# Side work of a hybrid Fourier and neighbourhood-attention block: stepped three times where it was four times, and two MLP weight jobs moved to the last gates

## The chip, the cores and the metric

The kernel runs on one core of a Trainium2 chip. The metric is device time in microseconds (us) of one execution; the time before is the median of three runs. TensorE is called PE, its weight loads PEld, VectorE DVE, ScalarE ACT, GpSimd POOL and SyncE SP. SP computes nothing: it issues most of the DMAs, one after the other, and each of them waits at the head of that queue for what it needs.

## The reference, cut to what matters

One transformer-like layer over 2048 latent tokens of width 1024, with 256 context tokens. Six modulation rows come from `silu(c) @ w_ada + b_ada` (and a second set from `c_ctx` for the context tokens).

```python
hx = modulate(rms_norm(x, norm1_g), sh1, sc1)        # hc: the same for ctx
f, q, k, v = split_projection(hx @ w_in)             # four parts of 512 columns
y_four = fourier_mix(f)                              # 2-D FFT over tokens and channels
y_attn = neighbourhood_attention(q, k, v, kc, vc, rpb)
mixed  = gated_merge(hx, y_four, y_attn, w_gate, w_fo, w_ao, w_o)   # sigmoid(hx @ w_gate)
x = x + g1 * mixed
x = x + g2 * ((relu(modulate(rms_norm(x, norm2_g), sh2, sc2) @ w_mlp1) ** 2) @ w_mlp2)
```

`w_mlp1` is 1024 by 4096 and `w_mlp2` 4096 by 1024, 16 MB each in fp32.

## The kernel before, in words

fp32 products are made from fp16 halves: an operand is scaled and split into a high and a low fp16 part, and three products (high-high, high-low, low-high) are summed in PSUM (`mm3`, line 77; its matmuls all have line 82).

**The input stage** multiplies `hx` (four blocks of 512 tokens, kept in SBUF) by `w_in` and `w_branch_gate`. Their columns come in units of 256, and the units in eight pairs (`seq`): pair 0 the Fourier columns f; pair 1 gates 4 and 5; pair 2 q0 with g0; pair 3 q1 with g1; pair 4 both v units; pair 5 k0 with g2; pair 6 k1 with g3; pair 7 the last gates, g6 and g7. `run_pair` (line 767) goes through a pair block by block, and for k and v through the context tokens too. Pair 3 begins with the building of `hc` from the context tokens. A gate or f unit makes two groups of 24 matmuls of 512 columns for each block, a q, k or v unit four groups of 24 matmuls of 256 columns. PSUM holds four such groups (`mmp`). A gate group is emptied by ACT (sigmoid, `ot_g`), a v group by ACT (`vo`, two buffers, stored to `vF`), a q or k group by ACT and DVE (norm and rotary: `ss`, `qn`, `t`, `qr`; POOL makes `rs`), then transposed on PE (`tq`) and split (`sH` on ACT, `sL` on DVE). The weights of the next pair are loaded and split beside the running one (`load_unit`).

**The side work** is written as Python generators whose steps are strewn between the groups. After every group `tick(share)` (line 457) adds `pace` to a counter, and for every 2 in the counter takes one step of each generator in `beside`:

```python
ticks[0] += pace[0]
with tc.issue_after(last_load[0].ins):
    while ticks[0] >= 2:
        ticks[0] -= 2
        for o in beside:
            if next(o, o) is o and o is side:
                blocks[2] = True
```

`issue_after` puts the DMAs of those steps behind the last load of x or of input weights in SP's queue; it orders nothing else. The order of instructions on every engine is made when the program is built: a scheduler goes by a simulated timeline, and takes the earliest in program order of those that it holds for ready. So a step can run ahead of, or behind, the group that it was written beside.

`side_work` (line 294) makes these steps: eight blocks of the context's modulation rows, two steps each and one more (1 to 17), eight of the second modulation (18 to 33), eight chunks of the gates' rows g1 and g2 (34 to 49), three tables of the attention's bias (50 to 52: `wm`, `tT`), 32 loads of 1 MB of the MLP weights (`w12m`, 53 to 84), and two steps that make scales from them (`msd`, `msc`); the 87th call finds it at its end. A modulation block or chunk is a 1 MB load (`awt`, two buffers), eight or so DVE instructions (`ada_sum`, lines 274 to 277) and one or two small matmuls on PE (`adc`, `adm`, `adg`). Of the 32 loads `w12m`, which use the same two buffers, DVE takes the maximum of the first 16 (line 338), ACT the sum of squares of the other 16 (line 340).

When `side` is at its end, `tick` also adds up `share` (1.5 for a gate group, 0.8 for v, 0.6 for q or k) and for each whole 1 takes a step of `early_blocks`: MLP weight jobs by `prepare` (line 389). A job loads 1 MB of `w_mlp1` or `w_mlp2` (`raw`), forms seven sums and differences of its quarters (DVE, line 430), halves each into two fp16 parts (ACT line 386, DVE line 387, the tile `wo`) and stores 1.75 MB to `w1d` or `w2d` in DRAM: one step to begin with, seven for each job, and the call that finds the end. There are 32 jobs; `N_EARLY` of them, eight, are done here, four of `w_mlp1` and then four of `w_mlp2`, and the MLP stage does the other 24.

After pair 4 `split_values` (v split into halves, line 838, 19 calls) joins `beside`. Ahead of pair 7 what is left of all of these is run to its end, the buffers `pb` are given back, and `beside` becomes `fourier_prep` (line 866): tables and norms for the Fourier and output weights (`tw`, `wn`, through two buffers `wst`) and two folds of f, 25 steps and the call that finds the end. What pair 7 leaves of it is run behind the pair. Then come the channel and token DFTs, the attention, the output projection and the MLP.

Of the kernel before, what the change touches and what calls it, by code (L numbers as in the profile page):

```python
# [8 lines left out]
F32 = mybir.dt.float32  # L9
F32R = mybir.dt.float32r  # L10
F16 = mybir.dt.float16
# [11 lines left out]
KT = D // 128  # L23
# [40 lines left out]
def dit_block(ctx: ExitStack, tc: tile.TileContext, a, out, taps=None, upto=9):  # L64
    nc = tc.nc
    act, dve, pool, pe, sp = nc.scalar, nc.vector, nc.gpsimd, nc.tensor, nc.sync
# [110 lines left out]
    pa = sbuf("p1a", "right")  # L177
# [116 lines left out]
    def side_work():  # L294
# [75 lines left out]
        dve.tensor_scalar(out=AB2, in0=AB2, scalar1=msc[:, 1:2], scalar2=None, op0=ALU.mult)  # L370
        dve.tensor_scalar(out=g2r, in0=g2r, scalar1=msc[:, 4:5], scalar2=None, op0=ALU.mult)

    def early_blocks():

        yield from prepare(jobs[:N_EARLY], lambda n_: pb.tile([128, KT, 256], F32, tag="awt", name=n_, bufs=2).rearrange("p k n -> p (k n)"),
                           lambda n_: pb.tile([128, 2, 256], F32, tag="aacc", name=n_, bufs=2).rearrange("p a n -> p (a n)"),
                           lambda n_: pb.tile([128, D], F32, tag="xh", name=n_, bufs=5).bitcast(F16).rearrange("p (c n) -> p c n", c=2),
                           2, sp.dma_start, sp.dma_start)
        del jobs[:N_EARLY]


    prepared, N_EARLY = set(), 8
    jobs = [(kind, f + o) for f in range(0, FF // 128, 8) for kind in (1, 2) for o in range(0, 8, 2)]

    def halve(hi, lo, src, scale):
# [65 lines left out]
    beside, pace = [side], [0]  # L451

    ticks = [0]
# [3 lines left out]
    def tick(share):  # L457

        ticks[0] += pace[0]
        with tc.issue_after(last_load[0].ins):  # L460
            while ticks[0] >= 2:
                ticks[0] -= 2
                for o in beside:
                    if next(o, o) is o and o is side:
                        blocks[2] = True

            if blocks[2]:
                blocks[1] += share
                while blocks[1] >= 1.0:
                    blocks[1] -= 1.0  # L470
                    next(blocks[0], None)
# [217 lines left out]
    seq = [f_, g_[4:6], (q_[0], g_[0]), (q_[1], g_[1]), v_, (k_[0], g_[2]), (k_[1], g_[3]), g_[6:8]]  # L689
# [75 lines left out]
        return r  # L765

    def run_pair(n):
        pace[0] = 3 if n == len(seq) - 1 else (0, 3, 2)[min(n, 2)]
        wu, new = pair(n), [load_pair_unit(n + 1, u) for u in range(2)] if n + 1 < len(seq) else []
        js = [0, 1, "c", 2, 3] if n else [1, 2, 3]  # L770
        for j in js:
# [94 lines left out]
    def fourier_prep():  # L866
        fold(0)
        yield
        for i in range(4):
            tH, tL = (fb.tile([128, 4, 512], F32R, tag=f"t{o}{i}", name=f"t{o}{i}") for o in "HL")  # L870
            tabs.append((tH, tL))

            tw = pa.tile([128, 4, 512], F32, tag="wst", name=f"tw{i}", bufs=2)
            sp.dma_start(tw, a["seq"][i].rearrange("(j p) m -> p j m", p=128))
            for j in range(4):
                split_on((pool, dve)[j % 2], tH[:, j], tL[:, j], tw[:, j])
                yield
            for j in (2 * i, 2 * i + 1):
                w, k = ((a["w_attn_out"][0], j), (a["w_out"][0], j - 2), (a["w_fourier_out"][0], j - 6))[(j >= 2) + (j >= 6)]
                tn = pa.tile([128, 2, D], F32, tag="wst", name=f"wn{j}", bufs=2)  # L880
                sp.dma_start(tn, w[k * 256:(k + 1) * 256, :].rearrange("(k p) n -> p k n", p=128))
                tn = tn.rearrange("p k n -> p (k n)")
                act.activation(tn, tn, AF.Square, accum_out=wn[:, j:j + 1])
                yield
        fold(1)

    for n in range(len(seq)):
        if n == 1:
# [6 lines left out]
        if n == len(seq) - 1:  # L895
# [7 lines left out]
            fb = sbuf("ffb")  # L903
# [960 lines left out]
```

## Time and profile before

| | |
|---|---|
| median of 3 runs | 2662.83 us (2658.7 to 2666.41) |
| the profiled execution | 2660.88 us, of which the span from first to last instruction is 2659.1 us |
| busy, share of the span | PE 2538.6 us (95%), DVE 1827.3 (69%), ACT 1183.3 (44%), POOL 484.4 (18%) |
| granted PE clock, mean | 0.985 |
| input stage, pairs 1 to 7 | about 157.6 to 838 us of the span |
| DFTs, attention and the rest | 838 to 2659.1 us |

All times of single instructions below are from that one profiled execution. An engine's idle time counts only where PE, or what ends last, waits for it. A "tick" below is one call of `tick`, so one group of matmuls.

### The profile page before, as it was taken

The page shows a single profiled execution, that of the slowest core. Times are in us where ns is not written, and L with a number is a line of the kernel's source. Part 1 is how long each engine was busy: PE and PEld are TensorE (multiplying, and loading weights), DVE is VectorE, ACT ScalarE, POOL GpSimd, SP SyncE. Part 2 cuts the span into 40 slices and gives each one's busy share as a digit, 9 for nine tenths or more (in the row PEclk, how much of TensorE's full clock was granted, in tenths as well). Part 3 has the DMA queues.
Part 4 walks back from the last instruction along what each step waited for, and adds up shares of the span by engine and source line. Part 5 has one row for each costly group of instructions (what it writes and reads, how often), then busy time and mean ns, then how long its engine had stood idle before and what let it go on. Part 6 is the DMA issues. An engine that isn't in the chain of part 4 may idle for free.

```text
span 2659.1 us, 42665 instructions
## 1 busy us (share of the span) xinstructions
PE 2538.6 (95%) x15830; PEld 1473.0 (55%) x15830; DVE 1827.3 (69%) x3672; ACT 1183.3 (44%) x2113; POOL 484.4 (18%) x715
## 2 busy tenths in 40 slices
PE   6899989898999899998999999999999999999999
PEld 5445756776656678875666444444444444444444
DVE  6756976568553678887777696978877644636367
ACT  5623225545242577874444564627351333314050
POOL 1201221012224545452000121121211100000000
PEclk9999999999999999998999999999999999999999
DMA  8577689867374744556767777787766533333334
GB/s 269 137 225 204 203 248 304 270 204 245 93 249 141 199 118 138 148 169 207 237 226 264 260 242 261 231 279 233 268 235 230 181 99 105 101 103 99 104 103 155
DMA packets 345962, 517.77 MB, mean 195 GB/s; under 512 B 48497, under 2 KB 210505, under 8 KB 341401
## 3 DMA queue, kind: packets, MB, share of 16 engines
q1 hardware_dynamic: 296425, 406.50, 48.8%
q0 software_dynamic: 29104, 75.23, 8.4%
q10 hardware_dynamic: 20224, 33.31, 3.9%
q8 instruction: 124, 2.03, 0.3%
q14 instruction: 85, 0.70, 0.1%
HBM read 370.11 MB, written 145.84 MB: 194 GB/s over the span
## 4 chain that ended last, share of the span: by engine, by line
PE 68%; DMA 11%; DVE 11%; issue 3%; ACT 3%; POOL 3%; SPq 2%; DVEq 0%; ACTq 0%; POOLq 0%
PE p L82 21%; PE pm L82 17%; PE ps_g L82 8%; PE po L82 6%; DMA w12m<-in_w_mlp 3%; PE pua L82 2%; PE ps_k L82 2%; PE tp L1325 2%; PE pmf L1263 2%; PE pv L1339 1%; SPq L188 1%; PE ps_f L82 1%; PE ps_v L82 1%; PE sc L1303 1%; DVE wo L387 1%
## 5 line engine op out<-in xcount | busy, mean ns | idle before, releaser
L82 PE MATMUL pm<-hc,wb 128*128 128x512 f16 x2688 | 582.6, 379 | 5.6 <-DVE p L1605 2.1
L82 PE MATMUL p<-wb,a 128*128 128x512 f16 x2688 | 581.9, 379 | 2.1 <-DVE X L1605 1.5
L82 PEld LDWEIGHTS <-wb 128*128 128x128 f16 x2688 | 262.9, 98 | 323.6 <-issue 7.3
L82 PEld LDWEIGHTS <-a 128*128 128x128 f16 x2688 | 263.0, 98 | 319.7 <-issue 2.9
L82 PE MATMUL ps_g<-hx,w_g 128*128 128x512 f16 x1536 | 342.5, 380 | 0.9 <-ACT ot_f L516 0.9
L1605 DVE TENSOR_TENSOR X<-X,p 128x512 f32<-128x512 f32 x280 | 184.5, 685 | 171.1 <-PE p L82 151.8
L82 PEld LDWEIGHTS <-hx 128*128 128x128 f16 x2304 | 227.4, 99 | 39.6 <-issue 7.2
L82 PEld LDWEIGHTS <-w_g 128*128 128x128 f16 x1536 | 151.0, 99 | 171.2 <-issue 3.2
L1091 POOL DMA_DIRECT2D bt<-tT x264 | 132.4, 508 | 76.3 <-DVE ri L1332 53.0
L1605 DVE TENSOR_TENSOR u<-pm,u 128x512 f32<-128x512 f32 x128 | 87.5, 690 | 84.3 <-PE pm L82 82.5
L1312 DVE CUSTOM_DVE_ANT_0 s<-sc,bt,qsc 128x736 f32<-128x736 f32 (+5 forms) x128 | 111.2, 869 | 37.1 <-PE sc L1306 33.9
L386 ACT ACTIVATE wo<-ws,msc 128x512 f16<-128x512 f32 x96 | 69.0, 718 | 152.0 <-DVE ws L430 124.0
L1609 ACT ACTIVATE p<-pm 128x512 f32<-128x512 f32 x32 | 18.9, 589 | 239.7 <-PE pm L82 239.7
L1739 POOL DMA_DIRECT2D xr<-x1d x32 | 17.3, 539 | 569.8 <-DVE X L1605 562.1
L1333 DVE SCALAR_TENSOR_TENSOR pL<-tp,pH 128x640 f16<-128x640 f32 (+1 forms) x128 | 112.3, 878 | 5.0 <-ACT pH L1328 4.5
L1316 ACT ACTIVATE s<-s,m 128x736 f32<-128x736 f32 (+5 forms) x128 | 104.6, 817 | 16.5 <-DVE m L1312 13.9
L386 ACT ACTIVATE wo<-raw,msc 128x512 f16<-128x512 f32 x128 | 87.4, 709 | 52.0 <-DVE raw L430 17.8
L82 PE MATMUL po<-wouH,mH 128*128 128x512 f16 x256 | 97.3, 384 | 9.3 <-DVE ga L1383 9.3
L1325 PE MATMUL tp<-ident,s 128*128 128x128 f32 x704 | 103.1, 281 | 0.8 <-ACT s L1316 0.7
L516 ACT ACTIVATE ot_g<-ps_g,usc_g 128x512 f32<-128x512 f32 x64 | 43.4, 681 | 130.9 <-PE ps_g L82 117.6
L82 PE MATMUL po<-wouL,mH 128*128 128x512 f16 x256 | 98.8, 386 | 2.4 <-POOL wouL L1536 2.4
L387 DVE SCALAR_TENSOR_TENSOR wo<-raw,msc,wo 128x512 f16<-128x512 f32 x128 | 94.4, 748 | 8.0 <-ACT wo L386 7.9
(535 smaller groups left out, 4645.9 us busy)
## 6 DMA issues: line engine op xcount, KB each, us to landing
wb<-w1d SPq DMA_DIRECT2D x224, 256.0 KB
wb<-w2d SPq DMA_DIRECT2D x224, 256.0 KB
w12m<-in_w_mlp SPq DMA_DIRECT2D x32, 1024.0 KB
raw<-in_w_mlp ACTq DMA_DIRECT2D x24, 1024.0 KB
w1d<-wo POOLq DMA_DIRECT2D x84, 256.0 KB, 4.0
w2d<-wo POOLq DMA_DIRECT2D x84, 256.0 KB, 4.0
gT<-ot_g SPq DMA_DIRECT2D x64, 256.0 KB
hc<-hcd SPq DMA_DIRECT2D x14, 1024.0 KB
```

Source lines behind the costliest of these rows:

```text
L82: last_mm[0] = pe.matmul(ps, l, r, start=(start and i == 0), stop=(stop and i == n - 1))
L188: last_load[0] = sp.dma_start(dst, src)
L386: act.activation(hi, src, AF.Copy, scale=scale)
L387: dve.scalar_tensor_tensor(out=lo, in0=src, scalar=scale, in1=hi, op0=ALU.mult, op1=ALU.subtract)
L516: act.activation(o, ps, func, scale=scale)
L1091: load_(t[i * 16:(i + 1) * 16, :, off + j0 * w:off + (j0 + 8) * w], raw(tT[ct], (2 * hp * 15 + dr) * w, [[120 * w, 16], [15 * w, 2], [1, 8 ...
L1263: pe.matmul(ps, l, r, start=(i == 0), stop=(i == len(prods) - 1))
L1312: tail["dve"] = dve.tensor_tensor_reduce(out=s[:, :n], in0=sc, in1=bias, op0=ALU.add, op1=ALU.min, scale=qsc[:, 4:5], scalar=3.0e38, accum ...
L1316: tail["act"] = act.activation(s[:, :n], s[:, :n], AF.Exp, bias=m1[:, 0:1], scale=-1.0, accum_out=m1[:, 1:2])
L1325: tail["pe"] = pe.transpose(tp[:, i * 128:(i + 1) * 128], s[:, o:o + 128], ident)
L1333: tail["dve"] = dve.scalar_tensor_tensor(out=pL[:, :c], in0=tp[:, :c], scalar=PTOP, in1=pH[:, :c], op0=ALU.mult, op1=ALU.subtract)
L1605: last["dve"] = dve.tensor_tensor(out=o, in0=x, in1=y, op=op)
```

## The change

The counter now takes 4 for a step, with `pace` 6, 3 and 8 where it was 3, 2 and 3. So pair 1 keeps three steps in two ticks, pairs 2 to 6 go from one step per tick to three in four ticks, and pair 7 from three in two ticks to two per tick. `N_EARLY` goes from 8 to 6. The two jobs that this takes away, both of `w_mlp2`, are done by the new generator `late_blocks` at the end of `fourier_prep`, through other buffers (`wst`, a new `ws`, and `w` with four products to a store in place of two).

```diff
+    def late_blocks():
+
+        yield from prepare(jobs[:2], lambda n_: pa.tile([128, KT, 256], F32, tag="wst", name=n_, bufs=2).rearrange("p k n -> p (k n)"),
+                           lambda n_: fb.tile([128, 512], F32, tag="ws", name=n_),
+                           lambda n_: pa.tile([128, 2, KT, 256], F16, tag="w", name=n_, bufs=4).rearrange("p o k n -> p (o k n)").rearrange("p (c n) -> p c n", c=4),
+                           4, sp.dma_start, sp.dma_start)
+        del jobs[:2]
+
     def early_blocks():
...
-    prepared, N_EARLY = set(), 8
+    prepared, N_EARLY = set(), 6
...
         ticks[0] += pace[0]
         with tc.issue_after(last_load[0].ins):
-            while ticks[0] >= 2:
-                ticks[0] -= 2
+            while ticks[0] >= 4:
+                ticks[0] -= 4
                 for o in beside:
...
     def run_pair(n):
-        pace[0] = 3 if n == len(seq) - 1 else (0, 3, 2)[min(n, 2)]
+        pace[0] = 8 if n == len(seq) - 1 else (0, 6, 3)[min(n, 2)]
...
                 act.activation(tn, tn, AF.Square, accum_out=wn[:, j:j + 1])
                 yield
         fold(1)
+        yield
+        yield from late_blocks()
```

## Rows read from the trace of the kernel before

**Rows 1.** The page: busy time of PE, and the shares by engine of the chain that ended last.

```profile
PE 2538.6 (95%) x15830; PEld 1473.0 (55%) x15830; DVE 1827.3 (69%) x3672; ACT 1183.3 (44%) x2113; POOL 484.4 (18%) x715
...
PE 68%; DMA 11%; DVE 11%; issue 3%; ACT 3%; POOL 3%; SPq 2%; DVEq 0%; ACTq 0%; POOLq 0%
```

**Rows 2.** Busy time by stretch: pairs 2 to 7, the DFTs, and all behind them. Columns: stretch and its length, then busy us and instructions of PE, PEld, DVE, ACT and POOL, the granted PE clock, the share of the DMA engines and their GB/s.

```profile
244.30:336.00 91.70, 91.70 (x646) 64.38 (x645) 84.40 (x279) 29.93 (x69) 20.54 (x18) 1.00 0.73 213
336.00:448.80 112.80, 95.24 (x632) 63.16 (x631) 86.47 (x197) 44.87 (x93) 22.20 (x22) 0.95 0.87 271
448.80:555.90 107.10, 98.59 (x878) 86.29 (x877) 53.14 (x127) 60.98 (x96) 3.18 (x5) 0.98 0.82 272
555.90:660.70 104.80, 96.13 (x664) 66.18 (x663) 81.31 (x208) 48.17 (x90) 20.96 (x18) 0.97 0.66 211
660.70:754.00 93.30, 93.30 (x669) 65.78 (x668) 55.23 (x168) 30.11 (x59) 21.34 (x22) 1.00 0.40 128
754.00:838.00 84.00, 84.00 (x398) 38.99 (x396) 26.02 (x41) 34.16 (x50) 17.95 (x15) 1.00 0.63 210
838.00:890.00 52.00, 49.63 (x259) 40.58 (x258) 26.75 (x69) 10.48 (x30) 36.09 (x59) 0.87 0.64 174
```

**Rows 3.** What PE waited for, in pair 3 (three rows), pair 4 (one) and pair 5 (two): us in total, times, longest us.

```profile
PE tq_q L603 <- DVE qr_q L588: 8.7, 4, 5.4
PE tq_q L603 <- DVE sL_q L610: 4.2, 2, 2.1
PE tp_c L229 <- ACT ht_c L235: 3.2, 2, 2.6
...
PE ps_v L82 <- ACT vo_v L646: 6.5, 4, 3.7
...
PE pu_g L494 <- DVE usc_k L495: 4.2, 1, 4.2
PE ps_k0c L82 <- DVE qn_k L577: 3.0, 1, 3.0
```

**Rows 4.** What DVE waited for in pair 3 (first row) and ACT in pair 4 (two rows), same columns.

```profile
DVE w1m L338 <- DMA w12m<-in_w_mlp: 18.7, 13, 3.1
...
ACT w12m L340 <- DMA w12m<-in_w_mlp: 13.2, 8, 4.1
ACT vo_v L646 <- DMA vF<-vo_v: 13.2, 7, 4.6
```

**Rows 5.** All instructions on the tile `w12m`: duration in ns (least, median, most), start of the first and of the last in us.

```profile
L338 DVE TENSOR_REDUCE w1m<-w12m x16: 2281/2286/2287, 335.0 to 413.3; 128x1 f32<-128x2048 f32 x16
...
L340 ACT ACTIVATE w12m<-w12m x16: 1903/1910/1912, 418.1 to 486.8; 128x2048 f32<-128x2048 f32 x16
```

**Rows 6.** The longest wait of PE in pair 3, in order of time on SP, DVE and PE (start us, us, instruction, in brackets the idle time before it and what ended it), and a later gate group on PE.

```profile
374.01 4.68 SPq L333 DMA_DIRECT2D w12m<-in_w_mlp  x2
...
376.04 2.29 DVE L338 TENSOR_REDUCE w1m<-w12m 128x1 f32<-128x2048 f32 x1 [3.10 <-DMA w12m<-in_w_mlp]
...
379.08 0.66 PE L603 MATMUL tq_q<-ident,qr_q 128*128 128x128 f32 x2 [5.36 <-DVE qr_q L588]
379.53 6.68 PE L82 MATMUL ps_g<-hx,w_g 128*128 128x512 f16 x24
...
391.73 5.34 PE L82 MATMUL ps_g<-hx,w_g 128*128 128x512 f16 x24
```

**Rows 7.** Where side steps ran: the matmul of the last chunk of g2 (PE), the first job `w12m` (DVE), the 20th and the 24th (ACT).

```profile
340.11 0.60 PE L313 MATMUL adg<-aaccg,ones 128*128 128x256 f32 x2
...
334.97 2.29 DVE L338 TENSOR_REDUCE w1m<-w12m 128x1 f32<-128x2048 f32 x1 [0.76 <-DMA w12m<-in_w_mlp]
...
428.26 1.91 ACT L340 ACTIVATE w12m<-w12m 128x2048 f32<-128x2048 f32 x1 [0.27 <-DMA w12m<-in_w_mlp]
...
450.94 1.91 ACT L340 ACTIVATE w12m<-w12m 128x2048 f32<-128x2048 f32 x1 [0.38 <-DMA w12m<-in_w_mlp]
```

**Rows 8.** The DVE work of the eight chunks of g1 and g2: durations in ns, first and last start.

```profile
L276 DVE SCALAR_TENSOR_TENSOR aaccg<-awtg,sil,aaccg x48: 462/480/489, 272.7 to 333.4; 128x256 f32<-128x256 f32 x48
...
L274 DVE TENSOR_SCALAR aaccg<-awtg,sil x16: 330/348/352, 272.0 to 327.6; 128x256 f32<-128x256 f32 x16
```

**Rows 9.** The eight early weight jobs, by their tile `raw`: halving on ACT and on DVE, a sum on DVE, and the loads of the four jobs of `w_mlp1` and of `w_mlp2`.

```profile
L386 ACT ACTIVATE wo<-raw,msc x32: 705/707/722, 498.2 to 667.7; 128x512 f16<-128x512 f32 x32
L387 DVE SCALAR_TENSOR_TENSOR wo<-raw,msc,wo x32: 742/746/752, 499.3 to 669.6; 128x512 f16<-128x512 f32 x32
L430 DVE TENSOR_TENSOR ws<-raw,ws x12: 678/686/691, 504.7 to 668.0; 128x512 f32<-128x512 f32 x12
...
L398 SPq DMA_DIRECT2D raw<-in_w_mlp x4: 373/426/488, 485.3 to 516.8; - x4
...
L400 SPq DMA_DIRECT2D raw<-in_w_mlp x4: 372/372/535, 581.2 to 635.9; - x4
```

**Rows 10.** Ten us of pair 5, columns as in rows 2.

```profile
640.00:650.00 10.00, 10.00 (x46) 5.85 (x47) 10.00 (x32) 6.55 (x10) 2.54 (x2) 0.75 0.26 96
```

**Rows 11.** The end of pair 7: its last 30 us (columns as in rows 2), the last of the norms `wn` on ACT, and the first DVE instruction of the DFT.

```profile
808.00:838.00 30.00, 30.00 (x146) 14.22 (x143) 0.00 (x0) 7.64 (x12) 0.77 (x1) 1.00 0.25 95
...
811.82 1.91 ACT L883 ACTIVATE wn<-wn 128x2048 f32<-128x2048 f32 x1 [2.77 <-DMA wn<-in_w_fourier_out]
...
840.22 0.16 DVE L949 COPY col<-pss 128x2 f32<-128x2 f32 x1 [33.59 <-PE pss L948]
```

## The prediction

> **What bounds the kernel now.** I read the page first: PE is busy for 95% of the span and holds 68% of the chain that ended last; DMA and DVE hold 11% each [rows 1]. A change that leaves PE's work alone can win only where PE stands idle or runs slowly, so the second view is the table by stretch [rows 2]. Pairs 2, 6 and 7 have PE busy for their whole length. The idle time of the stage that the change touches lies in pair 3 (112.80 - 95.24 = 17.6 us), pair 4 (107.10 - 98.59 = 8.5) and pair 5 (104.80 - 96.13 = 8.7). Behind the stage nothing is edited, and the attention needs the DFTs, so what the stage wins or loses ahead of 838 us I carry one to one to the end.
>
> The third view is that of the waits. In pair 3 PE waits in front of transposes for DVE (qr_q, sL_q) and for ht_c [rows 3]. Of DVE's own waits in the same stretch, 18.7 us are for the 1 MB loads `w12m` [rows 4]. The timeline shows the two joined: SP issues a load at 374.01, DVE stands 3.10 us before its maximum, which starts at 376.04 and takes 2.29, and PE, having waited 5.36 us, goes on at 379.08 [rows 6]. So the chain is load, maximum, rotary, transpose: DVE keeps its order, and an early place for the maximum holds up work for PE. The gate group behind that wait took 6.68 us where a later one took 5.34 [rows 6]: at 1.2 GHz for a part of it, then at 2.4. In pair 4 the same loads make ACT wait 13.2 us, the stores of v another 13.2, and PE waits 6.5 us for `vo`, which is queued behind them [rows 3, 4].
>
> **The change part by part.** First the steps. By the count before, 24 steps fall in pair 1, 24 in pair 2, 24 in pair 3 and 15 in pair 4 (87 calls); after, 24, 18, 18 and 27 (36 ticks by three quarters), so that `side` ends with the last tick of pair 4. Jobs `w12m` are steps 53 to 84: 20 in pair 3 and 12 in pair 4 before, 8 and 24 after. But the rows show a lead over the count: the 20th is due at the end of pair 3, 448.8, and ran at 428.26; the 24th is due four ticks on, near 460, and ran at 450.94 [rows 7]. The loop has no matmul, so nothing ties it to PE. What does tie its start is the chunks of g1 and g2 before it, whose matmul `adg` stands in PE's order: the last is step 49, the first tick of pair 3, and ran at 340.11, with the first maximum at 334.97 [rows 7]. After the change that step is the seventh of pair 3, tick 9.3 of 24, so the loop starts some 35 us later, and with a lead as before about 13 of its 32 jobs, not 8, still fall in pair 3.
>
> Pair 2: six steps fewer; PE has no idle time to lose there: 0.
>
> Pair 3: it loses 3 to 8 of its 16 maxima on DVE and gains three chunks. A maximum is 2.29 us [rows 5], by busy time 35.5 / 16 = 2.2; a chunk is 6 x 0.48 + 2 x 0.35 = 3.6 us [rows 8]. DVE's work goes from 86.5 us [rows 2] to 86.5 - 35.5 + 10.8 + (8 to 13) x 2.2 = 79 to 90 us, on about 94 us of PE work. Pair 2 carries 84.4 of DVE in 91.7 with no idle PE [rows 2], though without context tokens and with no maximum that waits. The building of `hc`, in the first third, now runs beside chunks, and the waits move to the later part. Bounds: at best all 17.6 us go and 1.3 us of slow clock (6.68 - 5.34), together 18.9; at worst 13 jobs wait as before, 13 x 18.7 / 16 = 15 us on top of 90, which is 105 of DVE in a stage of 112.8, and about nothing is won. I take 13 won, nearer the first end, since the 5.36, the longest wait, falls in the part with `hc`.
>
> Pair 4: 11 to 16 more jobs, to 19 or 24. All 16 of ACT are now here, where 9 were. Scaled, PE's wait becomes 6.5 x 16 / 9 = 11.6, or 5 more; but the stores of the four `w_mlp1` jobs, whose loads begin at 485.3 [rows 9], now come behind the pair, and they share the DMA engines with the stores of v: 2 less. I take 3 lost. Bounds: 6.5 won if the slower steps let `vo` through, 21 lost by the sum in the second rival.
>
> Pairs 5 and 6: the six early jobs get 0.8 + 22.8 + 22.8 = 46.4 shares for their 44 calls, so they end just ahead of pair 7, if no lead brings them forward (the eight of before were through at 669.6 [rows 9], in the first tenth of pair 6). The two `w_mlp2` jobs that go were in pair 5; the four `w_mlp1` jobs come in from pair 4. A job is 7 x 0.75 + 4 x 0.69 = 8.0 us of DVE and 7 x 0.71 = 5.0 of ACT [rows 9]. DVE is full at 640 to 650, where the clock is 0.75 [rows 10], and that stall (4.2 us of PE, for usc_k behind the halving [rows 3]) should shrink, while the start of the pair gets fuller. Bounds: 8.7 won; one job's 8.0 lost. I take 2 won. `split_values`, now 19.5 of its 19 calls in pair 5, costs nothing, as pair 6 has DVE at 55 of 93 us.
>
> Pair 7: `fourier_prep` is stepped faster, but in the trace it waits for its loads (ACT waited 2.77 us for the last norm, at 811.82), so it ends where it did. The two late jobs then have the last 24 to 30 us before the DFTs: DVE busy 0.00 and ACT 7.6 of 30, DMA share 0.25 [rows 11]. They need 16 us of DVE, 10 of ACT, 2 MB in and 3.5 MB out, at 210 GB/s [rows 2] 27 us. What hides them is the last six gate groups, whose results ACT empties in time from four banks; their issues stand in SP's queue among the stores of the gates. If that cover is gone, the first DVE instruction of the DFT at 840.22 is late by up to the 16 us. The pair's own drain behind it holds ten more calls by the count, two thirds of the work. DVE sat 33.59 us before 840.22 [rows 11], so I take 0.
>
> Sum, on the profiled execution: -13 + 3 - 2 + 0 = -12, so 2660.9 - 12 = 2648.9 us. The median lies 1.95 above that execution (2662.83 - 2660.88), so 2651 us.
>
> **The rivals.** *The pace doesn't bite.* The scheduler fills DVE's gaps with whatever is ready, and the lead [rows 7] shows that the loop goes by its loads; then pair 3 keeps its waits, later in the pair. For it: four `w_mlp1` jobs loaded by 516.8 [rows 9], well ahead of their shares. Against it: the start of the loop is tied to PE. Pair 3 then wins 4, pair 4 loses 3: 2660, or 2662 on the median.
>
> *Pair 4 becomes bound by its loads; slower.* The 31 intervals from the first to the last job are 151.8 / 31 = 4.9 us each [rows 5]. If the lead is lost, 24 jobs fall in pair 4: 24 x 4.9 = 118, and four groups more at 98.6 / 36 = 2.74 each make 129 where it was 107.1, so 21 lost. With 13 won in pair 3 and 2 in pair 5 that is 6 lost: 2667, on the median 2669. It decides above (32 x 2.74 + four banks, 11) / 24 = 4.1 us per job; in pair 4 the loads came at 272 GB/s in all [rows 2]. Against it: the lead, and the last nine jobs of before, from 450.94 to 486.8 [rows 5, 7], were 4.5 apart and cost 6.5.
>
> *The loads keep up.* Steps further apart let each load land before its turn: pair 3 wins 18.9, pair 4 6.5 and pair 5 2, which gives 2633.5, on the median 2635. Against it: DMA was already at 0.87 of its time in pair 3 [rows 2], and the bytes of the stage are the same. The Trainium skill ("HBM Reference", Specifications) says that a core that streams alone reaches well above its half share, about 425 GB/s; by it, as an estimate, a load of 1 MB comes every 2.5 us and this rival would hold. The trace disagrees: no stretch of the table has more than 272 GB/s [rows 2].
>
> **How the numbers follow.** Forecast 0.44 (own range 2643 to 2659), no bite 0.25, loads bind pair 4 0.17, loads keep up 0.14. A difference of 0.3%, 8 us, is about what a measurement tells from no change. Faster than that: 0.44 x 0.7 + 0.14 + 0.25 x 0.1 = 0.47; slower: 0.17 x 0.75 + 0.25 x 0.15 + 0.44 x 0.02 = 0.18; the rest, 0.35, within. The range reaches over half of the third rival and most of the second: 2637 to 2672.
>
> **What would show it.** Right: the first maximum `w1m` near 370, DVE's waits for `w12m` in pair 3 well under 18.7 us, pair 3 below 102 us, pair 4 near 110, and PE without idle time up to the DFTs with the late jobs done before them. Wrong: as many waits in pair 3 as before (no bite); more than 11 jobs' worth of ACT waits and pair 4 above 118 (the slower rival); or halving on DVE behind 840, with PE waiting for gL.

## The result, and the profile after

The changed kernel takes 2668.24 us (median of 19 runs, 2659.2 to 2676.51) where the kernel before took 2661.93 (19 runs beside them): a ratio of 1.0023, with a 95% interval of 1.0012 to 1.0034. That is 6 us more. It lies within the 0.3% that the prediction called no change, but on the other side: 12 us less were forecast, with a range of 2643 to 2659 for that forecast, and 2637 to 2672 for all its cases together. The profiled execution has a span of 2667.3 us, 8.2 above that of before.

The page's line of busy times: PE's busy time is what it was (2538.6 [rows 1]), and the end is later.

```profile
PE 2537.9 (95%) x15830; PEld 1473.5 (55%) x15830; DVE 1825.6 (68%) x3672; ACT 1183.6 (44%) x2113; POOL 484.5 (18%) x715
```

The stretches, with the columns of [rows 2], cut at the first matmul of each pair, and for the DFTs 1 us behind theirs, as before: pair 2, pair 3, pair 4, pairs 5 to 7, the DFTs.

```profile
241.90:336.00 94.10, 94.10 (x673) 66.64 (x672) 80.40 (x270) 33.77 (x72) 23.12 (x21) 1.00 0.63 185
336.00:442.80 106.80, 92.96 (x604) 60.77 (x603) 83.44 (x196) 27.73 (x74) 18.79 (x18) 0.95 0.68 213
442.80:557.40 114.60, 98.17 (x876) 85.38 (x875) 32.25 (x81) 58.52 (x85) 3.64 (x5) 1.00 0.78 258
557.40:838.50 281.10, 273.12 (x1729) 170.48 (x1727) 190.00 (x471) 128.44 (x224) 61.35 (x55) 0.99 0.66 218
838.50:894.90 56.40, 51.07 (x260) 42.11 (x259) 26.67 (x69) 10.97 (x32) 35.96 (x59) 0.82 0.66 179
```

Against [rows 2]: pairs 2 and 3 together went from 204.5 to 200.9 us, pair 4 from 107.1 to 114.6, pairs 5 to 7 from 282.1 to 281.1, the DFTs from 52.0 to 56.4. So 3.6 us were won, 7.5 lost, 1.0 won and 4.4 lost. Another 2.4 us were gained ahead of pair 2, where the change does nothing, and 2.9 lost between the DFTs and the output projection, where it does nothing either; in the runs below that part takes 290 to 295 us whatever was edited, so I count both as the spread of one execution. The questions are what pair 4 lost, what the DFTs lost, and why pair 3 won so little.

What PE waited for in pair 3 (first two rows) and in pair 4 (five); then DVE on loads in pair 3 (two rows), and ACT in pair 4 on its loads and on the stores of `vo` (us in total, times, longest us). Rows 3 and 4 have waits of before.

```profile
PE tq_q L611 <- DVE qr_q L596: 5.5, 3, 4.6
PE tp_c L229 <- DVE ht_c L233: 3.5, 1, 3.5
...
PE ps_v L82 <- ACT vo_v L654: 7.0, 7, 1.7
PE ps_v L82 <- ACT vo_v0c L654: 2.9, 2, 1.7
PE ps_v L82 <- ACT vo_v1c L654: 1.8, 2, 1.4
PE ps_v0c L82 <- ACT vo_v L654: 1.8, 2, 1.5
PE ps_v1c L82 <- ACT vo_v L654: 1.7, 1, 1.7
...
DVE w1m L338 <- DMA w12m<-in_w_mlp: 14.3, 8, 4.4
DVE aaccg L311 <- DMA br<-in_b_ada: 6.0, 1, 6.0
...
ACT w12m L340 <- DMA w12m<-in_w_mlp: 23.6, 15, 2.4
...
ACT vo_v L654 <- DMA vF<-vo_v: 8.0, 3, 5.2
ACT vo_v L654 <- DMA vF<-vo_v1c: 5.2, 2, 3.6
```

In pair 4 PE's waits for `vo` sum to 15.2 us, where they were 6.5 [rows 3]; these 8.7 us more cover the whole loss of the pair. The timeline shows how one of them is made. It is 10 us of pair 4 on ACT, SP and PE (start us, us, instruction, in brackets the idle time before it and what ended it):

```profile
481.33 1.91 ACT L340 ACTIVATE w12m<-w12m 128x2048 f32<-128x2048 f32 x1 [1.94 <-DMA w12m<-in_w_mlp]
483.24 0.45 ACT L654 ACTIVATE vo_v<-ps_v,usc_v 128x256 f32<-128x256 f32 x1
483.36 0.37 SPq L335 DMA_DIRECT2D w12m<-in_w_mlp  x1
...
485.85 1.91 ACT L340 ACTIVATE w12m<-w12m 128x2048 f32<-128x2048 f32 x1 [2.15 <-DMA w12m<-in_w_mlp]
487.75 0.46 ACT L654 ACTIVATE vo_v<-ps_v,usc_v 128x256 f32<-128x256 f32 x1
488.26 2.78 PE L82 MATMUL ps_v<-w_v,hx 128*128 128x256 f16 x24 [1.74 <-ACT vo_v L654]
489.12 1.91 ACT L340 ACTIVATE w12m<-w12m 128x2048 f32<-128x2048 f32 x1 [0.90 <-DMA w12m<-in_w_mlp]
```

Each `vo` of 0.45 us stands behind a square of 1.91 us, and each square behind a load that it waits 1 to 2 us for. The load issued at 483.36, as its buffer came free, is used at 489.12. A group of v needs 2.78 us of PE, a square every 4.0 us sets the pace. All instructions on the tile `w12m` give that spacing:

```profile
L338 DVE TENSOR_REDUCE w1m<-w12m x16: 2262/2286/2289, 354.3 to 454.4; 128x1 f32<-128x2048 f32 x16
...
L340 ACT ACTIVATE w12m<-w12m x16: 1909/1910/1912, 459.7 to 519.6; 128x2048 f32<-128x2048 f32 x16
```

The 16 squares run from 459.7 to 519.6, 59.9 / 15 = 4.0 us apart; of before seven had run in pair 3 [rows 5, 7]. A 1 MB load each 4.0 us is 262 GB/s, most of the 303 GB/s that was moved in those 59.9 us.

The second loss is at the first DFT. First two rows of before: PE's wait for `gL` there (us in total, times, longest us), and the last gate, which ACT empties as soon as PE has its group. Then rows of ACT, SP, DVE and PE after, as above:

```profile
PE pc L939 <- DVE gL L90: 1.0, 1, 1.0
...
837.25 0.69 ACT L516 ACTIVATE ot_g<-ps_g,usc_g 128x512 f32<-128x512 f32 x1 [4.49 <-PE ps_g L82]
...
834.13 2.64 SPq L412 DMA_DIRECT2D w2d<-wo  x2
...
834.86 0.72 ACT L394 ACTIVATE wo<-ws,msc 128x512 f16<-128x512 f32 x1 [1.42 <-DVE ws L438]
835.49 1.25 ACT L524 ACTIVATE ot_g<-ps_g,usc_g 128x512 f32<-128x512 f32 x2
835.62 0.75 DVE L395 SCALAR_TENSOR_TENSOR wo<-ws,msc,wo 128x512 f16<-128x512 f32 x1 [0.79 <-ACT wo L394]
836.86 7.25 SPq L525 DMA_DIRECT2D gT<-ot_g  x3
837.50 2.79 PE L949 MATMUL pc<-chan,fold 128*128 128x65 f32 x24
...
843.07 0.69 ACT L524 ACTIVATE ot_g<-ps_g,usc_g 128x512 f32<-128x512 f32 x1 [6.33 <-DMA gT<-ot_g]
844.07 1.09 DVE L90 TENSOR_TENSOR gL<-pc,gH 128x256 fp32r<-128x256 f32 x3 [3.19 <-ACT gH L87]
844.97 2.37 PE L949 MATMUL pc<-chan,fold 128*128 128x64 f32 x10 [4.29 <-DVE gL L90]
```

It is to be read from below. PE waits 4.29 us for `gL` (1.0 before), which waits for `gH` on ACT, which stands behind the last gate's `ot_g`. That one waits 6.33 us for a store of an earlier gate to free its buffer; `ot_g` has two. The gate in question was emptied only at 835.49, though PE had ended its group at 827.3, 8.2 us sooner: ACT had the halvings of the late job ahead of it. Its store was issued at 836.86, where it could have been at 836.16, since the second store of the late job stood ahead of it in SP's queue until its last product was halved (835.62, for 0.75). So SP's queue cost 0.7 us, and ACT's order the 8.2. In the runs below, every kernel with late jobs emptied that gate 5.0 to 8.5 us behind its group, every kernel without them 0.1 us behind. The wait is 3.3 us longer than before, most of the 4.4 lost; PE's own busy time grew by 1.4 (51.07 against 49.63 us), at a granted clock of 0.82 where it was 0.87.

### The profile page after: what moved, and what is told of

Read it like the earlier page. It is cut to its first block, busy times and chain, and to the rows that moved or that the text cites. A ratio compares the mean times of both kernels' runs of the same rounds, so it can differ in the third digit from the quotient of the medians.

```text
span 2667.3 us, 42653 instructions
## 1 busy us (share of the span) xinstructions
PE 2537.9 (95%) x15830; PEld 1473.5 (55%) x15830; DVE 1825.6 (68%) x3672; ACT 1183.6 (44%) x2113; POOL 484.5 (18%) x715
## 4 chain that ended last, share of the span: by engine, by line
PE 67%; DMA 11%; DVE 9%; issue 3%; ACT 2%; POOL 2%; SPq 1%; ACTq 0%; DVEq 0%; POOLq 0%
PE p L82 21%; PE pm L82 19%; PE po L82 6%; PE ps_g L82 6%; DMA w12m<-in_w_mlp 3%; PE pua L82 2%; PE tp L1335 2%; PE pmf L1273 2%; PE pv L1349 1%; PE ps_k L82 1%; PE ps_q L82 1%; DVE wo L395 1%; DMA raw<-in_w_mlp 1%; PE ps_v L82 1%; PE sc L1313 1%
## 5 line engine op out<-in xcount | busy, mean ns | idle before, releaser
L1326 ACT ACTIVATE s<-s,m 128x736 f32<-128x736 f32 (+5 forms) x128 | 104.5, 816 | 17.9 <-DVE m L1322 15.2
L82 PE MATMUL po<-wouH,mL 128*128 128x512 f16 x256 | 98.1, 384 | 0.0
```

Source lines behind the costliest of these rows:

```text
L82: last_mm[0] = pe.matmul(ps, l, r, start=(start and i == 0), stop=(stop and i == n - 1))
L1326: tail["act"] = act.activation(s[:, :n], s[:, :n], AF.Exp, bias=m1[:, 0:1], scale=-1.0, accum_out=m1[:, 1:2])
```

## The experiments

All ratios are to the kernel before, run beside each kernel, with 95% intervals. The lengths of stages are read from the first and last matmuls on their tiles in one profiled execution each; the DFTs, from the first `pc` to the last `psq`, so measured took 52.6 us before and 56.9 after. One execution is good to a few us: pairs 5 to 7 took 280 to 286 us over these runs. Nor is the profiled execution the median one: with the pace alone it lies 7 us above the median, with `vo` on DVE 10 us below. So the stages show where time went, and only the ratios say how much a run won or lost.

**The pace alone.** Eight early jobs, no late ones.

```diff
-    prepared, N_EARLY = set(), 6
+    prepared, N_EARLY = set(), 8
...
-        pace[0] = 8 if n == len(seq) - 1 else (0, 6, 3)[min(n, 2)]
+        pace[0] = 6 if n == len(seq) - 1 else (0, 6, 3)[min(n, 2)]
...
-        yield
-        yield from late_blocks()
```

> The slower pace alone: eight early jobs as before, no late jobs, the last pair stepped as before (6 of 4). Theory A (the loss has two places, pair 4 and the start of the DFTs, and the pace causes only the first): pairs 2 and 3 take 3 to 4 us less than before, pair 4 takes about 114 us, with PE waiting some 15 us for `vo`, and the first DFT matmul waits for nothing behind the last gates (4.29 us after the change); the last `eL` matmul comes 3 to 5 us sooner than after the change and the run ends 0 to 4 us above the kernel before. Rival B (the late jobs are the whole loss, pair 4 only gives back what pair 3 won): the time is at or below that of before, by up to 3 us. Rival C (the late jobs cost nothing on their own and the later start of attention comes from the pace): the DFT is as late as after the change, and the run ends 6 us above before.

Measured: 2669.79 us, ratio 1.0031 (1.0018 to 1.0043). The stretch of pair 4:

```profile
448.40:562.20 113.80, 99.55 (x877) 86.20 (x876) 31.62 (x78) 57.53 (x84) 2.53 (x4) 0.99 0.76 256
```

Pair 4 lost 6.7 us, with 13.6 us of waits of PE for `vo`, and the DFTs (53.0 us, PE's wait for `gL` 1.0) lost nothing, as theory A has it. B falls. C falls in the profile, for the wait at the first DFT goes with the late jobs; in the time it doesn't, for this run lost no less than the changed kernel. And A missed in part: pairs 2 and 3 won nothing here (205.0 us), pairs 5 to 7 took 285.4 us, with a wait of 5.2 for `usc_k` (4.2 before), and the run is 8 us above before, more than A allowed.

**The late jobs alone.** One step per tick in pairs 2 to 6, as before.

```diff
-        pace[0] = 8 if n == len(seq) - 1 else (0, 6, 3)[min(n, 2)]
+        pace[0] = 8 if n == len(seq) - 1 else (0, 6, 4)[min(n, 2)]
```

> Six early jobs and the two late ones, with the pace of before in pairs 2 to 6 (one step for each matmul group) and 8 of 4 in the last pair. Theory A: pair 3 and pair 4 are as before (about 113 and 107 us, 9 of ACT's squares in pair 4), the DFT still starts late, with the 6.3 us wait of `ot_g` for the gates' stores behind the store of the late jobs, and the last `eL` matmul comes some 4 us later after the last gate than before; the run ends 3 to 6 us above before. Rival B: the whole 6 us are here. Rival C: the time of before.

Measured: 2665.05 us, ratio 1.0010 (0.9995 to 1.0024). Pair 4, and PE's wait at the DFT:

```profile
450.10:557.90 107.80, 97.28 (x879) 85.62 (x878) 54.32 (x132) 61.34 (x98) 3.35 (x5) 1.00 0.83 270
...
PE pc L949 <- DVE gL L90: 2.0, 1, 2.0
```

Pair 4 is that of before; the DFTs took 55.3 us, 2.7 more, with the wait for `gL` at 2.0 instead of 4.29. In the time, late jobs alone aren't told apart from no change. The two parts, 1.0031 and 1.0010, don't add up to the 1.0023 of both, but the difference is within what three such intervals allow.

**The late jobs' stores on POOL.**

```diff
-                           4, sp.dma_start, sp.dma_start)
+                           4, sp.dma_start, pool.dma_start)
```

> The changed kernel with one edit: the late jobs' stores are issued by POOL and no longer by SP; loads, halving and all else stay. Theory (SP's queue): the store of the second late job stood at the head of SP's queue until its last product was halved, and the stores of the last gates stood behind it; with it on POOL `ot_g` no longer waits 6.3 us, PE's 4.29 us before the second group of the DFT go, and the run ends 3 to 5 us below the changed kernel, that is 1 to 3 above before. Rival (the DMA engines or DVE are simply late with 16 us more work): the gates' stores land as late as after the change, `ot_g` waits 4 us or more, and the time is that of the changed kernel.

Measured: 2669.58 us (7 runs), ratio 1.0029 (1.0013 to 1.0044). In order of time: two gates emptied on ACT, the last gate, and PE behind the first DFT group.

```profile
841.17 1.25 ACT L524 ACTIVATE ot_g<-ps_g,usc_g 128x512 f32<-128x512 f32 x2
...
846.41 0.69 ACT L524 ACTIVATE ot_g<-ps_g,usc_g 128x512 f32<-128x512 f32 x1 [4.00 <-PE pss L958]
...
848.30 5.94 PE L949 MATMUL pc<-chan,fold 128*128 128x64 f32 x32 [1.96 <-DVE gL L90]
```

The edit did what it should to the queue: a gate's store is now issued 0.03 us after the gate is emptied, where it was 0.70. But the gate itself is emptied as late as ever, 8.2 us behind its group on PE (841.17 for 832.9), and the last `ot_g` still waited 4.00 us, the sign that was set for the rival. PE's wait for `gL` fell from 4.29 to 1.96 and the DFTs from 56.9 to 53.5 us, but with these stores on SP the waits for `gL` came to 1.0 us in the run with half loads, 2.0 in the run before this one and 4.6 in the first run with the swap, so 1.96 is no gain that one execution can show. The gain of 3 to 5 us in the time did not come: the interval covers that of the changed kernel. The theory of SP's queue falls; what holds the gates back is ACT's order.

**The stores of `vo` on POOL.**

```diff
-            sp.dma_start(vF[tt + i, :, u * 256:(u + 1) * 256], vo)
+            pool.dma_start(vF[tt + i, :, u * 256:(u + 1) * 256], vo)
```

> The changed kernel with one edit: the stores of `vo` in pair 4 are issued by POOL (3.6 us busy in that pair) and no longer by SP, where each stands behind the issue of a 1 MB load that waits for a buffer. Theory P (SP's order): ACT's waits for `vF` stores (13 us in pair 4) go, PE's waits for `vo` fall from 15 us to 5 or less, pair 4 takes 104 to 109 us, and the run ends 5 to 9 us below the changed kernel. Rival Q (ACT's own order: `vo` stands behind a square that waits for its load): the squares still wait 0.5 to 2.7 us each, PE's waits for `vo` stay above 10 us, pair 4 above 112 us, and the time is within 2 us of the changed kernel.

Measured: 2667.17 us, ratio 1.0011 (1.0001 to 1.0022). ACT's and PE's waits in pair 4:

```profile
PE ps_v L82 <- ACT vo_v L654: 10.3, 4, 5.0
...
ACT vo_v L654 <- DMA vF<-vo_v: 9.3, 3, 5.2
```

Theory P falls: ACT still waits 14.5 us in all for these stores (13.2 in the changed kernel), PE 14.8 for `vo`, and pair 4 took 117.2 us. The squares' waits for their loads are 27.0 us. The stores are not held by SP's queue. The Trainium skill ("DMA: Bandwidth & Descriptors", Issuing engines are not separate DMA queues) says that transfers of all issuers interleave on the same 16 engines, and another issuer saves no more than issuing time; these waits agree.

**`vo` on DVE.** This and the next set ACT's order against the loads' bytes.

```diff
-            act.activation(vo, ps, AF.Copy, scale=und)
+            dve.tensor_scalar(out=vo, in0=ps, scalar1=und, scalar2=None, op0=ALU.mult)
```

> The changed kernel with one edit: in pair 4 DVE, not ACT, scales `ps_v` into `vo` (DVE is busy for 32 of the 115 us there); the loads, ACT's squares and the stores stay as they are. Theory Q (ACT's order: `vo` stands behind a square that waits for its 1 MB load): PE's waits for `vo` fall from 15 us to 3 or less although the squares wait for their loads as before (20 us or more), pair 4 takes 100 to 106 us, and the run ends 6 to 12 us below the changed kernel, so 0 to 6 below before. Rival R (DMA: the stores of `vo` land late whoever fills it, and two `vo` buffers hold PE up): DVE now waits for `vF` stores (13 us), PE waits 8 us or more for it, pair 4 stays above 110 us, and the time is that of the changed kernel.

Measured: 2666.31 us, ratio 1.0005 (0.9991 to 1.0020). Pair 4, then waits in it:

```profile
PE ps_v L82 <- DVE vo_v L654: 1.7, 3, 0.9
...
ACT w12m L340 <- DMA w12m<-in_w_mlp: 32.4, 16, 4.8
...
DVE vo_v L654 <- DMA vF<-vo_v: 20.8, 10, 3.1
...
445.00:551.00 106.00, 98.53 (x879) 86.59 (x877) 47.35 (x116) 44.45 (x49) 3.52 (x5) 0.98 0.82 278
```

The squares wait longer for their loads than in the changed kernel, 32.4 us against 23.6, and PE hardly waits: 3.3 us for `vo` in all. Pair 4 took 105.9 us, 8.7 less. Theory Q holds in the profile: the loads are late in both kernels, and what costs is what stands behind them on ACT. In the time, about 5 us of it are seen (1.0005 against 1.0023), short of the 6 to 12 expected, and the intervals overlap. Two more runs below have `vo` on DVE: over the three, pair 4 took 105.9 to 111.6 us, with 3.3 to 6.0 of waits for `vo`, and over four with `vo` on ACT and whole loads (the changed kernel and three runs above) 113.3 to 117.2, with 13.1 to 15.2. So the gain in the pair is real, and 8.7 us is the best of three.

**Half loads.** Half of `w_mlp2` is left out of the sum that sets its scale.

```diff
-                sp.dma_start(wt.rearrange("p (k n) -> p k n", k=2),
-                             a["w_mlp2"][0, j * 256:(j + 1) * 256, :].rearrange("(k p) n -> p k n", p=128))
+                wt = wt[:, :1024]
+                sp.dma_start(wt, a["w_mlp2"][0, j * 256:j * 256 + 128, :])
```

> The changed kernel with the 16 loads for ACT's squares cut to half a megabyte each (half of w_mlp2 is left out of the sum that sets its scale), in the same order on the same engines. Theory Q: a square waits because its load takes about 4 us and only two are under way; with half the bytes ACT's waits for `w12m` fall from 24 us to 8 or less, PE's waits for `vo` from 15 to 4 or less, and pair 4 takes 100 to 105 us. Rival S (it is ACT's own busy time or the order of squares and `vo`, not the bytes): a square takes 1.0 us where it took 1.9, but PE still waits 8 us or more and pair 4 takes 108 us or more.

Measured: 2666.64 us, ratio 1.0010 (0.9995 to 1.0025); pair 4 took 108.8 us, and PE waited 9.2 us for `vo`. ACT on the tile, and its waits:

```profile
L340 ACT ACTIVATE w12m<-w12m x16: 1047/1057/1057, 461.3 to 505.2; 128x1024 f32<-128x1024 f32 x16
...
ACT w12m L340 <- DMA w12m<-in_w_mlp: 20.8, 14, 2.0
```

None of theory Q's signs came, and all of S's did, the last two narrowly. Pair 4 won 5.8 us; whether by the bytes or by the shorter squares (1.06 us for 1.91), this edit can't tell, as it cuts both. With half the bytes the squares run 43.9 / 15 = 2.9 us apart, not 2.0, and still wait 20.8 us: with two buffers, each square can start only when the load that was issued two squares ago is in.

**`vo` on DVE in the kernel before.** The edit is that of the run with `vo` on DVE, made to the kernel before.

> The kernel before with the same edit as the run beside it: `vo` is scaled by DVE. There DVE carries the halving of four early jobs in pair 4 (53 us busy of 107). Theory Q: PE's 6.5 us of waits for `vo` in pair 4 go only in part, since `vo` now stands behind halvings on DVE that wait for loads: pair 4 takes 102 to 108 us and the time is within 4 us of before. If ACT's order were the only cause, pair 4 would take about 100 us and the time be 6 us below before. If DVE's order is as bad as ACT's, pair 4 takes 108 us or more.

Measured: 2669.23 us, ratio 1.0023 (1.0010 to 1.0036). Pair 4 took 108.9 us, and PE waited for the scales of the loop instead:

```profile
PE pmb L352 <- DVE msd L349: 5.3, 1, 5.3
```

`msd` is DVE's too, and DVE now waits 10.6 us for the loads of the halvings and 24.0 for stores of `vo`. PE's waits for `vo` fell from 6.5 to 1.9 us, and those for `msd` took their place: DVE's order is there as bad as ACT's, the third of the cases expected. The pair explains 1.7 of the 6 us lost; this execution lost the rest in pairs 2 and 3 (3.0) and 5 to 7 (5.0), where no `vo` is made, and stands 5 us above the median. So what the edit costs there is measured, and why is only in part shown.

**`vo` on DVE, no late jobs.** The changed kernel with the two lines of `late_blocks()` in `fourier_prep` taken out, and `vo` on DVE.

> The changed kernel with `vo` on DVE and without the two late jobs (six early ones; the other jobs fall to the later stage, which prepares what is left). If the two causes are ACT's order in pair 4 and the late jobs at the DFTs, both are gone here: pair 4 takes 100 to 106 us, the DFTs take 53 us, and up to the attention the run is 10 to 14 us ahead of the changed kernel. If the two jobs are hidden in the later stage, the time is 3 to 8 us below before; if not, they cost there what they save, and it ends 0 to 4 us below before.

Measured: 2666.21 us, ratio 1.0011 (0.9996 to 1.0026). Pair 4 took 107.9 us and the DFTs 54.8; the MLP stage, which got the two jobs, took 1177.7 us where all others take 1172.3 to 1173.6, but the output projection ahead of it (from the first `pua` to the last `po`) took 293.3 where the others take 296 to 302. Together they came to 1471.0 us, against 1471.7 in the run with the late jobs and `vo` on DVE. So taking the late jobs away shows no gain, in its time or in its stages; what they cost at the DFTs stays below what one execution tells. The run was expected 10 to 14 us ahead of the changed kernel up to the attention; at the end of the DFTs it was 2.6 ahead.

**A third `vo` buffer, with `vo` on DVE.**

```diff
-            vo = pb.tile([128, 256], F32, tag="vo", name=f"vo_{nm}", bufs=2)
+            vo = pb.tile([128, 256], F32, tag="vo", name=f"vo_{nm}", bufs=3)
```

> The changed kernel with `vo` scaled by DVE and three `vo` buffers where there were two. With two, the run with `vo` on DVE had pair 4 at 105.9 us, and DVE waited 31 us for the stores of `vo` before it could fill a buffer again, while PE waited 3.3 us for `vo`. If those stores are what still holds PE, a third buffer takes the rest: PE waits under 1.5 us for `vo`, pair 4 takes 101 to 104 us, and the run ends 2 to 5 us below the run with two buffers, 4 to 9 below the changed kernel. If what is left in pair 4 is the weights' own chain (`usc_k`, 2.8 us) and slow clock, pair 4 stays at 105 us or more.

Measured: 2666.40 us, ratio 1.0007 (0.9994 to 1.0021), the same as with two. In this execution pair 4 took 111.6 us, with 6.0 of waits for `vo` and 3.8 for `usc_k`. The buffers were not what was left; the second case expected, 105 us or more, came.

**Squares first, maxima last.** The order of the loop's two halves, with three `vo` buffers, and `vo` on ACT.

```diff
-        for i in range(32):
+        for i in (*range(16, 32), *range(16)):
...
-            vo = pb.tile([128, 256], F32, tag="vo", name=f"vo_{nm}", bufs=2)
+            vo = pb.tile([128, 256], F32, tag="vo", name=f"vo_{nm}", bufs=3)
```

> The changed kernel with the two halves of the weight loop in the other order, ACT's 16 squares first (pair 3) and DVE's 16 maxima last (pair 4), `vo` on ACT, and three `vo` buffers. If the mechanism is one of engine order (whoever waits for a 1 MB load holds what is queued behind it), pair 3 loses DVE's 14 us of waits for `w12m` and PE's waits for `qr_q` (5 to 8 us), since ACT has the slack there, and pair 4 loses PE's 15 us for `vo`, since only `vmax` stands behind the maxima: pairs 2 and 3 take 194 to 199 us, pair 4 101 to 106, and the run ends 8 to 15 us below the changed kernel, 2 to 9 below before. If the loads' bytes set the two stages, the waits move to `sH_q` on ACT and `vo`'s buffers: pairs 2 and 3 stay at 200 or more, pair 4 at 108 or more, and the time is within 3 us of the changed kernel.

Measured: 2658.24 us, ratio 0.9984 (0.9973 to 0.9995): 4 us less than before by the ratio, and 10 less than the changed kernel. Waits of PE and DVE in pair 4, and the stretches of pair 3 and pair 4:

```profile
PE ps_v L82 <- ACT vo_v L654: 2.3, 2, 2.0
...
DVE w1m L338 <- DMA w12m<-in_w_mlp: 26.6, 16, 3.2
...
336.00:447.00 111.00, 97.49 (x619) 65.74 (x617) 59.05 (x191) 57.14 (x107) 21.61 (x21) 0.91 0.77 241
447.00:548.00 101.00, 95.88 (x873) 85.05 (x872) 60.10 (x88) 28.93 (x55) 2.22 (x4) 1.00 0.79 257
```

Pair 4 is 13 us shorter than in the changed kernel, at much the same rate of 257 GB/s: DVE now waits 26.6 us for the same kind of load, and PE waits 3.2 for `vo`. Pairs 2 and 3 (203.5 us) did not win: `qr_q` no longer holds PE, but `ht_c` (4.8 us), `sL_q` (4.1) and the weights of v (`usc_v`, 3.2) do, and the granted clock of pair 3 is 0.91 (0.95 before and after), with PE busy 97.5 us (95.2 and 93.0). So the half of the expectation that spoke of pair 3 failed: taking the maxima's waits from DVE gave nothing back there; DVE waited 14.7 us for ACT's `sq_q` in their place. The DFTs took 59.7 us, the longest of all runs.

**The same swap in the kernel before.** Both edits of the run above.

> The kernel before (its pace, eight early jobs, none late) with the same two edits as the run beside it, squares first and three `vo` buffers. By engine order: pair 3 loses most of DVE's 18.7 us of waits for `w12m`, which are now ACT's, and takes 102 to 108 us where it took 112.8; pair 4 loses ACT's 13.2 us of waits and takes 102 to 106 us; the run ends 5 to 12 us below before. If the pace does matter once the order is right, it is 3 us or more above the run beside it; if the late jobs still cost their 3 to 4 us at the DFTs, it is below it by as much.

Measured: 2671.49 us, ratio 1.0022 (1.0011 to 1.0034). The stretch of pair 4:

```profile
449.00:559.00 110.00, 100.07 (x884) 87.57 (x883) 78.10 (x155) 44.66 (x82) 4.32 (x6) 0.97 0.82 269
```

Nothing of the 5 to 12 us expected came: pairs 2 and 3 took 203.7 us (204.5 before), and pair 4 got longer. Here the loop ends in pair 4 and early jobs begin in it, so DVE is busy 78.1 of 110 us, and PE waits for the scales (`pmb`, 4.2 us). At the pace of before, ACT does 28 halvings of early jobs in pair 4, in this run as in the kernel before and with the late jobs alone; at the slower pace it does none. Pace and late jobs together are worth 10 us under this order (0.9984 against 1.0022), where they cost 6 under the old one. The DFTs took 58.9 us in this run, without any late job, and 59.7 and 58.2 in the two others with the swap. So they get longer with the swap as well, and why stays open.

**The swap with two `vo` buffers.** The first of the two edits alone, in the changed kernel.

> The changed kernel with one edit, squares first and maxima last, and two `vo` buffers as in the changed kernel. With three, pair 4 took 101.5 us and the time was 0.9984 of before. If the order alone does it, PE waits under 5 us for `vo`, pair 4 takes 101 to 105 us and the ratio to before is 0.997 to 1.000. If the third buffer is needed (`vmax` behind a maximum that waits keeps a buffer, 1 to 3 us each), PE waits 8 us or more for `vo`, pair 4 takes 107 us or more, and the ratio is 1.001 or more.

Measured: 2661.59 us (11 runs), ratio 0.9993 (0.9981 to 1.0005). The stretch of pair 4:

```profile
444.50:547.90 103.40, 98.07 (x877) 86.37 (x876) 60.84 (x91) 30.23 (x56) 2.67 (x4) 0.98 0.77 255
```

PE waited 2.6 us for `vo` in it. The order does it: with this one edit the loss of pair 4 is gone, and the run is 8 us below the changed kernel, with intervals that don't touch. What the third buffer adds (0.9984) is not told apart from nothing, and with two the run isn't told apart from before.

## Why the prediction was wrong, point by point

**Pair 3: "I take 13 won" is the step that missed most.** Won were 3.6 us in pairs 2 and 3. The count held: 14 of the 32 jobs still fell in pair 3 (13 were reckoned), DVE's busy time was 83.44 (79 to 90), and its waits for the maxima's loads fell from 18.7 to 14.3. Three things were wrong with the 13.

- Fewer jobs meant little less waiting per job (14.3 / 14 = 1.0 against 18.7 / 16 = 1.2), and the one long wait that the 13 leaned on came back in another place: PE's longest for `qr_q` is 4.6 us where it was 5.4.
- The three chunks that came into the pair were priced at their 3.6 us of DVE each, with no wait. But a chunk has a small load too, `br`, a piece of `b_ada`. It was issued at 338.79 and used at 350.58, and DVE stood 6.05 us before it, beside the building of `hc`: PE's 3.5 us for `ht_c` are this wait (before, 3.2 us there stood behind ACT [rows 3]). Every run with the slower pace has such a wait of 5.0 to 7.9 us there, and no run with the pace of before. With it DVE waited 20.3 us for loads in pair 3, more than the 18.7 of before.
- Even without any of the maxima's waits the pair does not give its idle time back: in the three runs with the swap PE waits for `qr_q` hardly at all, and pairs 2 and 3 took 200.9 to 203.7 us. But there ACT's squares wait for loads in the pair; what a pair 3 without any late load would win, no run shows.

Seven more runs with the slower pace and the old order of the loop took 199.4 to 205.0 us in pairs 2 and 3, 201.5 on the mean, and three with the pace of before 204.5 to 207.5, 205.7 on the mean, so 4 us is the size. That is what the first rival, "the pace doesn't bite", gave pair 3. The pace did move the start of the loop (354.3, where it was 335.0 and 370 was named); within the loop the loads set the time. Pair 4 shows it too: squares and groups alternate one to one, where three steps in four ticks were written.

**Pair 4: "I take 3 lost" was mis-sized.** The step scaled PE's 6.5 us by 16 / 9 to 11.6 and took "2 less" because the loads of the early jobs leave the pair. The mechanism was the right one: all 16 squares came into pair 4 and `vo` stood behind them. But each cost 0.95 us (15.2 / 16) where 0.72 was carried over, and the 2 us of relief did not come, since the squares' own loads, one per 4.0 us, are what they wait for. The term is +7.5 where +3 stood. With the loop's halves in the other order it is gone, with the loads as late as ever. The second rival had this effect, at 21 us; its point of decision, 4.1 us per job against 4.0 measured, was nearly met, but only 18 of the 24 jobs it reckoned with were left for pair 4. That its time, 2669 us, is almost the one measured is luck: it adds 13 won and 21 lost, where 3.6 and 7.5 were measured.

**Pairs 5 and 6** were put at -2 and, with pair 7, came to -1, which the spread of 280 to 286 us over the runs can't confirm.

**Pair 7: "so I take 0" left out a cost at the first DFT.** The late jobs were done in time, as reckoned: their last halving is at 835.62, ahead of the DFT. What failed is "whose results ACT empties in time": with the late jobs' halvings ahead of them on ACT, the last gates were emptied 3.6 to 10.7 us behind their groups, and PE waited 4.29 us for `gL` where it had waited 1.0. The step named another cost, "their issues stand in SP's queue among the stores of the gates", which was 0.7 us. Over the runs with the old order of the loop, the DFTs took 53.5 to 56.9 us with late jobs (seven runs) and 52.6 to 54.8 without (four), so the 4.4 us of the first pair of profiles is the largest case, and about 2 the mean. In the time this could not be seen: 1.0010 for the late jobs alone holds 1.

**The sum.** -3.6 + 7.5 - 1.0 + 4.4 = +7.3 in the edited stretches of this execution, where -12 was forecast. The gain was a third of its size, the loss in pair 4 two and a half times, and the loss at the DFTs was put at nothing. The third rival, that steps further apart let loads keep up, was the farthest off: in pair 4 the loop ran at the rate of its loads with two buffers, and the squares still waited 23.6 us for them.

## What to carry to other kernels

Before moving a loop of loads, look at which instructions will be queued behind its waits on the engine that consumes them. In this kernel a load that was always late did little harm behind an engine that had nothing else to hand on: slower steps moved the loop from DVE beside q to ACT beside v, and lost; giving the wait in pair 4 to DVE, by running the two halves of the loop in the other order, took 8 to 10 us off the changed kernel, with the loads as late as before. The same swap in the kernel before lost 6 us, so it is no rule by itself. And side work that is finished in time can still delay what is queued behind it on its engine: the late jobs ended before the DFT, and the gates that ACT emptied behind them came 5 to 8 us late.

## What the runs showed that I had not expected

- Half the bytes did not halve the interval. A 1 MB load of pair 4 was used 5.8 us after its issue (483.36 to 489.12); half a megabyte, in the run with half loads, was issued at 480.26 and used at 484.83, 4.6 us later. With two buffers a loop over such loads ran at 262 GB/s with whole ones and at 0.52 MB / 2.93 us = 179 GB/s with halves. The Trainium skill ("DMA: Bandwidth & Descriptors", Anatomy of one DMA) gives a transfer issued by GpSimd a fixed part of about 2 us, and the rest by its bytes at 436 GB/s; as an estimate from that, the half load should be 1.2 us quicker. The two times above differ by as much, though SP issues these loads, and both lie 1.4 us above the page's figures (4.4 and 3.2).
- A wait that costs nothing can be large: DVE stood 31 us before the stores of `vo` in the run with `vo` on DVE, while PE waited 3.3 us for it.
- The worth of one edit changed sign with its neighbours: the change itself cost 6 us under the old order of the loop and won 10 under the new one, with intervals well apart. `vo` on DVE looks alike (+6 in the kernel before, about -5 in the changed kernel), but the -5 is not clear of noise.
